# Gate and up projection of two feed-forward stages by seven products of quarters

## The chip, the cores and the metric

The kernel runs on one core of a Trainium2 chip. The metric is the device time of one execution in microseconds (us); the time before is 2174.57 us, the median of three runs from 2169.86 to 2176.21. The engines of the core run side by side and each works through its own queue in order: TensorE (PE, the matmuls; PEld are its weight loads), VectorE (DVE), ScalarE (ACT), GpSimd (POOL) and SyncE (SP), which issues the loads.

## The reference

Three layers on 512 tokens of 1024 features in float32: a recurrent mixer and a feed-forward stage, an attention mixer and a feed-forward stage, then a block with a mixer of its own and a mixture of experts. The change concerns the two feed-forward stages (`layer` 0 and 1), with D_MODEL = 1024 and D_FF = 2816:

```python
def rmsnorm(x, g):
    xf = x.astype(jnp.float32)
    y = xf * lax.rsqrt(jnp.mean(xf * xf, axis=-1, keepdims=True) + EPS)
    return (y * g.astype(jnp.float32)).astype(x.dtype)

def swiglu(h, w_gu, w_down):
    u = h @ w_gu
    g, v = u[..., :D_FF], u[..., D_FF:]
    return (jax.nn.silu(g) * v) @ w_down
...
        h = h + swiglu(rmsnorm(h, norm_g[layer, 1]), ffn_w_gu[layer], ffn_w_down[layer])
```

## The kernel before

Activations lie transposed: eight tiles `h[k]` of 128 features by 512 tokens. Every product in float32 is made of three matmuls on parts: `split` (L422) makes a high part on ACT (a copy that rounds, L425) and a low part on DVE (the difference, L426), and `mm3` (L414) adds high x high, high x low and low x high into one PSUM bank. The gain of the norm is multiplied into the activations when they are split (`normed`, L634), the row factor `rbc` only after the product; its sum of squares is added up on POOL (`square_acc`, L437).

Weights come through `Stream`. `weight_order` lists the weight tiles of the whole kernel in the order of use, 1024 columns each (eight tiles of 128 x 128). `next` splits up to `ahead` = 3 tiles beyond the one in use (`_split`: high part `whi` on ACT at L271, low part `wlo` on DVE at L272, four buffers each) and loads two more; a load brings two tiles, 1 MB, into one of three `raw` buffers on SP's queue.

`ffn` (L789) works in two halves of 11 hidden tiles. For a tile `f`, `product` makes gate and up, 24 matmuls of 512 columns each. Then DVE multiplies both by `rbc` out of PSUM (L813, L816), ACT applies Silu, DVE multiplies them (L817), and `split` makes the parts `hidh` and `hidl`. After a half, its down projection follows: eight residual tiles of 33 matmuls (88 weight tiles), each added to `h[m]` on DVE (L826). The order on each engine comes from a scheduler that works from this code; waits are semaphores between the engines' queues.

Of the kernel before, what the change touches and what calls it, by code (L numbers as in the profile page):

```python
# [22 lines left out]
P = 128  # L23
T = 512
# [7 lines left out]
HF = 11  # L32
# [174 lines left out]

def ffn_layout(gu, dn):
    g = tiles_seq(gu, 0, D, 0, DFF)
    v = tiles_seq(gu, 0, D, DFF, 2 * DFF)  # L210
    return (np.stack([g, v], 1).reshape(2 * NF, P, 8 * P),
            np.concatenate([tiles_seq(dn, 0, HF * P, 0, D), tiles_seq(dn, HF * P, DFF, 0, D)], 0))

# [10 lines left out]
class Stream:  # L224
# [5 lines left out]
    def __init__(self, kb, order, ahead=3, raw_ahead=2):  # L230
        self.kb, self.order, self.ahead, self.raw_ahead = kb, order, ahead, raw_ahead
        self.raw, self.part = {}, {}
        self.stop = len(order) - KD
        self.i = self.ld = self.sp = 0

    def load(self, first=None, r=None):

        name, idx, _ = self.order[self.ld]
        src = self.kb.A[name]
        p, w = src.shape[1], src.shape[2]  # L240
        kb = self.kb
        n = 1
# [14 lines left out]
    def _split(self):  # L257
# [3 lines left out]
        name, idx, gain = self.order[self.sp]  # L261
        r = self.raw.pop(self.sp)
# [21 lines left out]

    def _ready(self, i):

        return self.order[i][0] not in self.LATE or i < self.ld

    def next(self, name):
        assert self.order[self.i][0] == name, (self.order[self.i], name)  # L290
        while self.sp < min(len(self.order), self.stop) and self.sp <= self.i + self.ahead and self._ready(self.sp):
            self._split()
        while self.ld < len(self.order) and self.ld <= self.i + self.ahead + self.raw_ahead and self._ready(self.ld):
# [93 lines left out]
class Kernel:  # L387
# [140 lines left out]

    def ffn_order(self, add, layer):
        for half in range(2):  # L530
            add(f"w_gu{layer}", 22 * half, 22 * half + 22)
            add(f"w_dn{layer}", 11 * half, 11 * half + 11)
# [255 lines left out]

    def ffn(self, layer, gain):  # L789
        nc, W = self.nc, self.W  # L790
        with ExitStack() as ctx:
            kp = ctx.enter_context(self.pool(f"fk{layer}"))
            wk = ctx.enter_context(self.pool(f"fw{layer}"))
            xs = self.normed(self.vec(gain), lambda: wk.tile([P, T], F32, name="fa", bufs=3))
            ssq, rbc = self.ssq, None
            for half in range(2):
                hid, banks = [], {}

                def product(f):
                    banks[f] = [self.bank() for _ in range(2)]  # L800
                    for o in banks[f]:
                        self.mm3(o, list(zip(W.tiles(f"w_gu{layer}", 8), xs)))

                for f in range(HF):
                    if f not in banks:
                        product(f)
# [1433 lines left out]
```

## Time and profile before

| | us |
|---|---|
| median of three runs | 2174.57 |
| the profiled execution, its own time | 2176.83 |
| its span | 2175.1 |
| PE busy | 2089.9 (96%) |
| DVE busy | 1069.7 (49%) |
| ACT busy | 789.2 (36%) |
| POOL busy | 295.9 (14%) |
| layer 0: gate and up, first half | 265.2 to 387.9 |
| layer 0: down, first half | 387.9 to 447.8 |
| layer 0: gate and up, second half | 447.8 to 568.6 |
| layer 0: down, second half | 568.6 to 628.5 |
| layer 1, the same four | 1077.6 to 1201.6, to 1261.5, to 1382.4, to 1442.3 |

A stage's place is read from the matmuls: those on `xh` and `xl` are gate and up, those on `hidh` and `hidl` the down projection. A matmul's record begins when it enters the array and ends when its result is there, so records overlap, and what a matmul costs is the distance to the next one's start. Of the other engines, an instruction that waits in front of its operands can stand in the trace with the wait in its record.

### The profile page before, as it was taken

To read this page: it belongs to the slowest core of one execution; us is meant where nothing else is said; L and a number is where in the kernel's file an instruction comes from. 1 tells how busy PE (TensorE), PEld (TensorE's weight loads), DVE (VectorE), ACT (ScalarE), POOL (GpSimd) and SP (SyncE) were. 2 spreads that over 40 slices of the span, in tenths; PEclk is the share of its full clock that TensorE was granted. 3 is DMA by queue.
4 is the path that set the end of the run, shared out by engine and by line. 5 is a ranking of instruction groups with operands and counts; after the bars stand their busy time and mean duration, and the time that the engine had idled before them with its cause. 6 is when DMAs were issued, how large, how long until landed. Compare 5 with 4: busy or idle time off the path is not lost. (4 is left out here: it accounts for less than half of the span.)

```text
span 2175.1 us, 25890 instructions
## 1 busy us (share of the span) xinstructions
PE 2089.9 (96%) x10282; PEld 1628.4 (75%) x10282; DVE 1069.7 (49%) x1928; ACT 789.2 (36%) x1188; POOL 295.9 (14%) x394
## 2 busy tenths in 40 slices
PE   7999999999999999999999999999999997998987
PEld 5777788888889978888778888888888885332456
DVE  6987744344457464555454344435664433212136
ACT  4675533223347533323432223343453221111223
POOL 2221200000013021211200000030110111111203
PEclk9999999999999999999999999999999998999999
DMA  5122342322224300101032222232211275999971
GB/s 182 47 96 78 120 152 96 107 97 97 88 66 136 133 35 15 40 20 40 19 109 94 97 97 97 88 116 87 88 59 65 97 307 199 371 420 417 380 289 39
DMA packets 71251, 281.72 MB, mean 130 GB/s; under 512 B 8859, under 2 KB 14235, under 8 KB 58452
## 3 DMA queue, kind: packets, MB, share of 16 engines
q1 hardware_dynamic: 60388, 264.63, 33.3%
q0 software_dynamic: 5504, 12.30, 1.5%
q10 hardware_dynamic: 5232, 3.07, 0.5%
q8 instruction: 83, 1.36, 0.2%
q14 instruction: 44, 0.36, 0.1%
HBM read 272.40 MB, written 15.73 MB: 132 GB/s over the span
## 5 line engine op out<-in xcount | busy, mean ns | idle before, releaser
L271 ACT ACTIVATE whi<-raw 128x1024 fp32r<-128x1024 f32 (+2 forms) x249 | 261.5, 1054 | 652.5 <-PE bank L418 587.5
L418 PE MATMUL bank<-xh,whi 128*128 128x512 f32 x1160 | 464.8, 401 | 10.5 <-ACT xh L428 7.6
L418 PE MATMUL bank<-xh,wlo 128*128 128x512 f32 x1160 | 459.1, 396 | 13.4 <-DVE wlo L272 13.3
L418 PE MATMUL bank<-xl,whi 128*128 128x512 f32 x1160 | 455.0, 392 | 0.0
L272 DVE TENSOR_TENSOR wlo<-raw,whi 128x1024 fp32r<-128x1024 f32 (+2 forms) x249 | 310.1, 1249 | 200.0 <-ACT whi L271 194.5
L418 PEld LDWEIGHTS bank<-xh,wlo 128*128 128x128 f32 x1160 | 219.9, 190 | 66.3 <-DVE wlo L272 15.8
L418 PEld LDWEIGHTS bank<-xh,whi 128*128 128x128 f32 x1160 | 220.8, 190 | 57.5 <-ACT xh L428 7.6
L418 PEld LDWEIGHTS bank<-xl,whi 128*128 128x128 f32 x1160 | 220.2, 190 | 49.5 <-issue 1.2
L445 POOL TENSOR_TENSOR ssq<-ssq,sq 128x512 f32<-128x512 f32 x27 | 40.2, 1489 | 791.5 <-ACT sq L432 791.5
L418 PE MATMUL bank<-hidh,whi 128*128 128x512 f32 x352 | 137.2, 390 | 0.0
L418 PE MATMUL bank<-hidh,wlo 128*128 128x512 f32 x352 | 137.1, 390 | 0.0
L418 PE MATMUL bank<-hidl,whi 128*128 128x512 f32 x352 | 137.1, 389 | 0.0
L2043 PE MATMUL bank<-rawa,xe 128*64 128x512 f32 x328 | 93.6, 627 | 9.9 <-DMA rawa<-w_eg 6.2
L432 ACT ACTIVATE prob<-bank 128x512 f32<-128x512 f32 (+1 forms) x96 | 57.1, 595 | 111.1 <-PE bank L1232 81.1
L816 DVE TENSOR_TENSOR fb<-bank,rows 128x512 f32<-128x512 f32 x44 | 30.4, 691 | 133.2 <-PE bank L418 133.2
L1215 PEld LDWEIGHTS acc<-v,prob 128*128 128x128 f32 x640 | 79.8, 192 | 6.2 <-POOL prob L1242 2.2
L1215 PE MATMUL acc<-v,prob 128*128 128x96 f32 x640 | 82.2, 275 | 1.4 <-POOL prob L1242 1.4
L418 PEld LDWEIGHTS bank<-hidl,whi 128*128 128x128 f32 x352 | 66.1, 188 | 13.9
L418 PEld LDWEIGHTS bank<-hidh,wlo 128*128 128x128 f32 x352 | 66.1, 188 | 13.7
L418 PEld LDWEIGHTS bank<-hidh,whi 128*128 128x128 f32 x352 | 66.1, 188 | 13.6
L813 DVE TENSOR_TENSOR fa<-bank,rows 128x512 f32<-128x512 f32 x44 | 30.4, 691 | 88.5 <-PE bank L418 88.5
L975 PE MATMUL bank<-whi,xh 128*128 128x512 f32 (+2 forms) x192 | 71.6, 373 | 0.0
(562 smaller groups left out, 3634.5 us busy)
## 6 DMA issues: line engine op xcount, KB each, us to landing
raw<-w_gu SPq DMA_DIRECT2D x44, 1024.0 KB, 4.8
rawa<-w_eg SPq DMA_DIRECT2D x41, 1024.0 KB, 13.9
raw<-w_dn SPq DMA_DIRECT2D x20, 1024.0 KB, 4.8
raw<-w_eg SPq DMA_DIRECT2D x16, 1024.0 KB, 13.5
rawa<-w_ed SPq DMA_DIRECT2D x16, 1024.0 KB, 14.6
raw<-w_mix SPq DMA_DIRECT2D x12, 1024.0 KB, 4.8
raw<-w_ed SPq DMA_DIRECT2D x10, 1024.0 KB, 15.7
rawb<-w_eg SPq DMA_DIRECT2D x7, 1024.0 KB, 16.9
```

The lines of the kernel that those rows point to most:

```text
L271: nc.scalar.activation(hi, r, AF.Copy)
L272: nc.vector.tensor_tensor(lo, r, hi.bitcast(F32), op=ALU.subtract)
L418: i = nc.tensor.matmul(o, a, b, start=first and n == 0, stop=last and n == N - 1)
L432: return self.nc.scalar.activation(o, i, f, **kw)
L445: self.nc.gpsimd.tensor_tensor(self.ssq, self.ssq, sq, op=ALU.add)
L813: nc.vector.tensor_tensor(a, og, rbc, op=ALU.mult)
L816: nc.vector.tensor_tensor(b, ov, rbc, op=ALU.mult)
L975: nc.tensor.matmul(banks[tt][:, :n], xh, wh, start=k == 0, stop=False)
L1215: i = nc.tensor.matmul(a[:, h * AW:h * AW + AW], e[:K, h * P:h * P + P], v, start=first and h == 0, stop=last and h == HPG - 1)
L2043: last = nc.tensor.matmul(o[s], xe[:, 4 * pi + k, s], w(k), start=pi == 0 and k == 0, stop=pi == 1 and k == 3)
```

## The change

Gate and up are computed for pairs of column tiles (256 columns of the weights) and pairs of feature tiles by one level of Strassen's algorithm in the form with seven products. The weight block of a feature pair and a column pair has four quarters A11, A12, A21, A22 of 128 x 128; the activations of a feature pair have four quarters of 128 features by 256 tokens, B11 to B22.

- `quarters` lays the weights out so that one load of 1 MB (`raw`, 2048 columns) brings the four quarters of a column pair, 512 columns each, for all four feature pairs.
- `operand_sums` makes four differences T1 to T4 of the activations on DVE, once a stage; the seven operands of each feature pair are split, 28 tiles (`xh`, `xl`, and twelve more, `xq`) instead of eight pairs. Before, the gain was multiplied in by `split`; now ACT makes a scaled copy first.
- `_quarter` makes four sums of weight quarters (`qsum`, S1 to S4) on POOL, with three buffers, and splits each of the seven operands, 512 columns, as before on ACT and DVE (L497, L498). `tno` numbers pairs of quarters, so that `ahead` = 3 counts three pairs, six products.
- `quarter_products` runs the seven products (12 matmuls of 256 columns each, four feature pairs by three parts), and combines them: two copies out of PSUM on ACT, five sums out of PSUM on DVE and two sums on POOL (L902). In a stage's first step, three products run on the first three feature pairs before the last pair is needed.
- In `ffn`, the gate's product with `rbc` moves from PSUM to SBUF on DVE (L987), the up's to POOL (L989).
- The hidden tiles come in chunks of 8, 8 and 6 (`CHUNKS`) instead of 11 and 11. `ffn_steps` puts the gate of the next pair ahead of a chunk's down projection; the last chunk's starts with the tiles that don't need the last pair (`down_tiles`, `LATE`).

```diff
+CHUNKS = (8, 8, 6)
+LATE = 3
...
 class Stream:
     def load(self, first=None, r=None):
...
+        if isinstance(gain, str):
+            if (name, idx) not in self.quarters:
+                r = kb.wp.tile([P, 2048], F32, name="raw", bufs=kb.RAW)
+                kb.nc.sync.dma_start(r, src[idx])
+                self.quarters[name, idx] = {c: r[:, 512 * i:512 * i + 512] for i, c in enumerate(("A11", "A12", "A21", "A22"))}
+            self.ld += 1
+            return
...
+    SUMS = {"S1": ("A21", "A22", ALU.add), "S2": ("S1", "A11", ALU.subtract), "S4": ("A12", "S2", ALU.subtract), "S3": ("A11", "A21", ALU.subtract)}
+
+    def _quarter(self, q, c):
+        kb, nc = self.kb, self.kb.nc
+        if c in self.SUMS:
+            a, b, op = self.SUMS[c]
+            q[c] = self.sums.tile([P, 512], F32, name="qsum", bufs=3)
+            nc.gpsimd.tensor_tensor(q[c], q[a], q[b], op=op)
...
+        kb.split(hi, lo, q[c])
...
     def next(self, name):
-        while self.sp < min(len(self.order), self.stop) and self.sp <= self.i + self.ahead and self._ready(self.sp):
+        while self.sp < min(len(self.order), self.stop) and self.tno[self.sp] <= self.tno[self.i] + self.ahead and self._ready(self.sp):
             self._split()
...
+    PRODUCTS = {"A11": "B11", "A12": "B21", "S1": "T1", "S2": "T2", "S4": "B22", "S3": "T3", "A22": "T4"}
+
+    def ffn_steps():
+        out, lo = [], 0
+        for c, n in enumerate(CHUNKS):
+            hi = (lo + n) // 2
+            out += [(x, j) for j in range(lo // 2, hi) for x in "gu" if (x, j) not in out]
+            if hi < NF // 2:
+                out.append(("g", hi))
+            out.append(("d", c))
+            lo += n
+        return out
...
+    def quarter_products(self, name, xs, wk, out, late):
...
+        for c in self.PRODUCTS:
...
+            if c in ("A11", "S1"):
+                m[c] = copied(o)
+            elif c == "A12":
+                sum_(o, m["A11"], x=a[0])
+            elif c == "S2":
+                m[c] = sum_(o, m["A11"])
+                m["U4"] = sum_(m[c], m["S1"], nc.gpsimd)
+            elif c == "S4":
+                sum_(o, m["U4"], x=a[1])
+            elif c == "S3":
+                m[c] = sum_(o, m["S2"])
+                sum_(m[c], m["S1"], nc.gpsimd, b[1])
+            else:
+                sum_(o, m["S3"], x=b[0])
...
     def ffn(self, layer, gain):
...
+            for j in range(KD // 2):
+                scaled = tiles("fa", 4)
+                for i in range(2):
+                    self.act(scaled[i], self.h[2 * j + i], AF.Copy, scale=g[:, 2 * j + i:2 * j + i + 1])
+                q = self.operand_sums(tiles("fb", 2), *scaled)
+                xs.append({})
+                for n in self.PRODUCTS.values():
+                    xs[j][n] = room.pop(0), room.pop(0)
+                    self.split(*xs[j][n], q[n])
+            for k in range(KD):
+                self.square_acc(k, self.h[k], lambda: wk.tile([P, T], F32, name="fa", bufs=4))
...
+                if kind == "u":
+                    for f, a, b in zip((2 * i, 2 * i + 1), gates.pop(i), out):
+                        nc.vector.tensor_tensor(a, a, rbc, op=ALU.mult)
+                        self.act(a, a, AF.Silu)
+                        nc.gpsimd.tensor_tensor(b, b, rbc, op=ALU.mult)
+                        nc.vector.tensor_tensor(a, a, b, op=ALU.mult)
+                        hid[f] = [kp.tile([P, T], FR, name=f"hid{x}", bufs=max(CHUNKS)) for x in "hl"]
+                        self.split(*hid[f], a)
```

The order on DVE in the middle of layer 0's gate and up, before: one hidden tile, with two weight tiles for a later one (`rows` is `rbc`).

```order
L813 TENSOR_TENSOR fa_2375<-bank_2315,rows_2223 128x512
L272 TENSOR_TENSOR wlo_2346<-raw_2279,whi_2345 128x1024
L816 TENSOR_TENSOR fb_2378<-bank_2316,rows_2223 128x512
L817 TENSOR_TENSOR fa_2375<-fa_2375,fb_2378 128x512
L272 TENSOR_TENSOR wlo_2388<-raw_2279,whi_2387 128x1024
L426 TENSOR_TENSOR hidl_2382<-fa_2375,hidh_2381 128x512
```

The same place of after on DVE: part of the step of an up product, with the low parts for the next step's gate and up among the sums out of PSUM (L902).

```order
L498 TENSOR_TENSOR wlo_3035<-qsum_3032,whi_3034 128x512
L498 TENSOR_TENSOR wlo_3035<-qsum_3038,whi_3034 128x512
L902 TENSOR_TENSOR fc_3054<-bank_3031,fc_3013 128x256
L990 TENSOR_TENSOR fa_2795<-fa_2795,fb_2938 128x512
L902 TENSOR_TENSOR fb_2939<-bank_3057,fc_3054 128x256
L498 TENSOR_TENSOR wlo_3091<-raw_2631,whi_3090 128x512
L498 TENSOR_TENSOR hidl_3076<-fa_2795,hidh_3075 128x512
L990 TENSOR_TENSOR fa_2796<-fa_2796,fb_2939 128x512
L498 TENSOR_TENSOR wlo_3091<-raw_2804,whi_3090 128x512
```

Two operations of 1024 columns have become low parts of 512, seven for a step, and the products with `rbc` and of gate and up now have both inputs in SBUF. POOL has nothing in this place before; what stands in its queue around layer 0's stage is this (the sums of squares of the stage, a clearing of a buffer, then the sums of squares after the stage):

```order
L445 TENSOR_TENSOR ssq_2064<-ssq_2064,fa_2078 128x512
L445 TENSOR_TENSOR ssq_2064<-ssq_2064,fa_2081 128x512
L569 MEMSET z_2022 128x1024
L570 DMA yd_104<-z_2022 128x8x1024
L445 TENSOR_TENSOR ssq_2064<-ssq_2064,fa_2084 128x512
L445 TENSOR_TENSOR ssq_4419<-ssq_4419,sq_4421 128x512
```

After, POOL in the middle of the gate and up of layer 0, nearly two steps:

```order
L334 TENSOR_TENSOR qsum_2991<-raw_2631 128x512
L334 TENSOR_TENSOR qsum_2997<-qsum_2991,raw_2631 128x512
L902 TENSOR_TENSOR fa_2796<-fc_2911,fc_2855 128x256
L334 TENSOR_TENSOR qsum_3032<-raw_2631,qsum_2997 128x512
L334 TENSOR_TENSOR qsum_3038<-raw_2631 128x512
L334 TENSOR_TENSOR qsum_3131<-raw_2804 128x512
L902 TENSOR_TENSOR fc_3015<-fc_3013,fc_2988 128x256
L989 TENSOR_TENSOR fb_2938<-fb_2938,rows_2485 128x512
L334 TENSOR_TENSOR qsum_3167<-qsum_3131,raw_2804 128x512
L334 TENSOR_TENSOR qsum_3173<-raw_2804,qsum_3167 128x512
L902 TENSOR_TENSOR fb_2939<-fc_3054,fc_2988 128x256
L989 TENSOR_TENSOR fb_2939<-fb_2939,rows_2485 128x512
```

Sums for a later step stand between those that combine this step's products, and each waits in its place. At the start of layer 0's stage, DVE now has this behind the last residual addition (`h7`), of which the last rows are the twelve low parts of the later operands:

```order
L837 TENSOR_TENSOR h7_83<-h7_83,bank_1962 128x512
L498 TENSOR_TENSOR wlo_2197<-raw_1756,whi_2196 128x512
L498 TENSOR_TENSOR wlo_2197<-raw_1805,whi_2196 128x512
L498 TENSOR_TENSOR xq0_2042<-fb_2106,xq0_2042 128x256
L498 TENSOR_TENSOR xq1_2043<-fb_2106,xq1_2043 128x256
...
L888 TENSOR_TENSOR fb_2130<-fa_2126 128x256
L888 TENSOR_TENSOR fb_2131<-fa_2127,fa_2126 128x256
L888 TENSOR_TENSOR fb_2130<-fa_2127,fb_2130 128x256
L498 TENSOR_TENSOR xq5_2047<-fa_2126,xq5_2047 128x256
...
L498 TENSOR_TENSOR xq11_2053<-fb_2131,xq11_2053 128x256
```

Before, one low part of 512 columns stood there. On POOL, the seven sums of squares of the stage have moved from between the residual additions to behind the last of them.

## Rows read from the trace of the kernel before

**Rows 1.** The page's first part: engine, busy us, share of the span, instructions.
```profile
PE 2089.9 (96%) x10282; PEld 1628.4 (75%) x10282; DVE 1069.7 (49%) x1928; ACT 789.2 (36%) x1188; POOL 295.9 (14%) x394
```

**Rows 2.** Stretches: length, then PE, PEld, DVE, ACT, POOL; clock, DMA, GB/s.
```profile
265.20:387.90 122.70, 122.70 (x540) 100.55 (x539) 55.55 (x71) 39.96 (x50) 3.80 (x4) 1.00 0.36 129
447.80:568.60 120.80, 120.80 (x529) 99.18 (x528) 54.22 (x64) 35.33 (x43) 0.00 (x0) 1.00 0.28 96
1077.60:1201.60 124.00, 122.89 (x539) 100.45 (x538) 60.01 (x74) 43.63 (x56) 10.87 (x7) 1.00 0.27 94
1261.50:1382.40 120.90, 120.90 (x530) 99.24 (x529) 54.22 (x64) 35.40 (x43) 0.00 (x0) 1.00 0.28 96
```

**Rows 3.** Timeline of PE in gate and up: start, length, instruction.
```profile
329.72 0.39 PE L418 MATMUL bank<-xl,whi 128*128 128x512 f32 x1
...
351.70 0.39 PE L418 MATMUL bank<-xl,whi 128*128 128x512 f32 x1
```

**Rows 4.** Timeline of PE, matmuls of 256 columns in two other places.
```profile
1505.57 0.28 PE L418 MATMUL bank<-rqh,rkh 128*128 128x256 f32 x1
1505.69 0.28 PE L418 MATMUL bank<-rql,rkh 128*128 128x256 f32 x1
...
1575.06 0.28 PE L1622 MATMUL bank<-whi,xh 128*128 128x256 f32 x1
...
1578.92 0.28 PE L1623 MATMUL bank<-wlo,xh 128*128 128x256 f32 x1
```

**Rows 5.** Groups by form: count | busy us, mean ns of one | idle before.
```profile
L271 ACT ACTIVATE whi<-raw 128x1024 fp32r<-128x1024 f32 x237 | 249.8, 1058 | 638.8 <-PE bank L418 582.5 <-issue 17.9 <-PE bank L977 14.1
L426 DVE TENSOR_TENSOR oTl<-bank,oTh 128x256 fp32r<-128x256 f32 x16 | 6.7, 417 | 11.1 <-ACT oTh L425 11.1
L1259 POOL TENSOR_TENSOR av<-av 128x256 f32<-128x256 f32 x15 | 11.0, 733 | 45.4 <-DVE av L1198 45.2
```

**Rows 6.** Timelines of POOL and DVE at the kernel's end (xN: merged).
```profile
2148.23 12.77 POOL L2214 TENSOR_TENSOR rawa<-rawa,rows 128x512 f32<-128x512 f32 x8 [16.38 <-ACT rows L432]
...
2149.56 3.46 DVE L2183 SCALAR_TENSOR_TENSOR raw<-raw,rawa 128x512 f32<-128x512 f32 x2 [4.01 <-POOL rawa L2214]
2152.95 3.49 DVE L2184 SCALAR_TENSOR_TENSOR raw<-raw,h 128x512 f32<-128x512 f32 x2
...
2163.52 1.29 DVE L2183 SCALAR_TENSOR_TENSOR raw<-raw,rawa 128x512 f32<-128x512 f32 x2 [0.17 <-ACT raw L432]
2164.73 1.29 DVE L2184 SCALAR_TENSOR_TENSOR raw<-raw,h 128x512 f32<-128x512 f32 x2
```

**Rows 7.** Timelines of POOL and DVE at the kernel's start.
```profile
17.38 1.29 POOL L445 TENSOR_TENSOR ssq<-ssq,y 128x512 f32<-128x512 f32 x1
19.34 4.83 POOL L445 TENSOR_TENSOR ssq<-ssq,y 128x512 f32<-128x512 f32 x3 [0.67 <-ACT y L432]
...
20.75 4.50 DVE L272 TENSOR_TENSOR wlo<-raw,whi 128x1024 fp32r<-128x1024 f32 x2
```

**Rows 8.** Timelines of POOL and DVE ahead of layer 0's feed-forward stage.
```profile
245.26 1.82 POOL L445 TENSOR_TENSOR ssq<-ssq,fa 128x512 f32<-128x512 f32 x1 [21.53 <-ACT fa L432]
...
244.69 1.23 DVE L272 TENSOR_TENSOR wlo<-raw,whi 128x1024 fp32r<-128x1024 f32 x1 [0.20 <-ACT whi L271]
245.84 0.68 DVE L744 TENSOR_TENSOR h<-h,bank 128x512 f32<-128x512 f32 x1
```

**Rows 9.** Timeline of all engines at the start of layer 0's stage.
```profile
265.42 0.69 DVE L744 TENSOR_TENSOR h<-h,bank 128x512 f32<-128x512 f32 x1 [1.21 <-PE bank L418]
...
267.74 1.59 POOL L445 TENSOR_TENSOR ssq<-ssq,fa 128x512 f32<-128x512 f32 x1
```

**Rows 10.** Timeline of PE behind a wait, ahead of layer 1's stage.
```profile
1064.03 0.44 PE L1263 MATMUL bank<-ident,av 128*128 128x128 f32 x2 [2.11 <-DVE av L1259]
...
1066.57 0.63 PE L418 MATMUL bank<-oTh,whi 128*128 128x512 f32 x1
1066.99 0.63 PE L418 MATMUL bank<-oTl,whi 128*128 128x512 f32 x1
```

More of the change, by code (lines that the diff above doesn't have):

```diff
@@ L232, in __init__ @@
         self.raw, self.part = {}, {}
+        self.tno, t, half = [], -1, False
+        for _, _, gain in order:
+            quarter = isinstance(gain, str)
+            t += not (quarter and half)
+            half = quarter and not half
+            self.tno.append(t)
+        self.quarters, self.sums, self.half = {}, None, None
         self.stop = len(order) - KD
@@ L236, in load @@
     def load(self, first=None, r=None):
-        name, idx, _ = self.order[self.ld]
+        name, idx, gain = self.order[self.ld]
         src = self.kb.A[name]
@@ L261, in _split @@
         name, idx, gain = self.order[self.sp]
+        if isinstance(gain, str):
+            return self._quarter(self.quarters[name, idx], gain)
+        self.half = None
         r = self.raw.pop(self.sp)
@@ new lines, in ffn, with tiles @@
+            W.sums = wk
+            def tiles(name, bufs):
+                return [wk.tile([P, T], F32, name=name, bufs=bufs) for _ in range(2)]
+            room = [self.xp.tile([P, T], FR, name=f"x{i}{k}") for k in range(KD) for i in "hl"]
+            room += [kp.tile([P, T], FR, name=f"xq{i}") for i in range(7 * KD // 2 - len(room))]
+            room = [x[:, hf * i:hf * i + hf] for x in room for i in range(2)]
+            g = self.vec(gain)
+            xs = []
+            for j in range(KD // 2):
[7 more added lines that the diff above has]
+                    self.split(*xs[j][n], q[n])
@@ new lines, in ffn @@
+            for k in range(KD):
+                self.square_acc(k, self.h[k], lambda: wk.tile([P, T], F32, name="fa", bufs=4))
+            ssq, rbc = self.ssq, None
+            gates, hid, lo = {}, {}, 0
+            for u, (kind, i) in enumerate(self.ffn_steps()):
+                if kind == "d":
+                    tl, bank = W.tiles(f"w_dn{layer}", KD * CHUNKS[i]), {}
+                    hi = lo + CHUNKS[i]
+                    for (k, m), wt in zip(down_tiles()[i], tl):
+                        if k == lo:
+                            bank[m] = self.bank()
+                        self.mm3(bank[m], [(wt, hid[k])], first=k == lo, last=k == hi - 1)
+                        if k == hi - 1:
+                            nc.vector.tensor_tensor(self.h[m], self.h[m], bank[m], op=ALU.add)
+                    lo = hi
+                    continue
+                out = tiles(*(("fa", 4) if kind == "g" else ("fb", 2)))
+                self.quarter_products(f"w_gu{layer}", xs, wk, out, u == 0)
+                if kind == "g":
+                    gates[i] = out
+                if u == 0:
+                    rcol = self.rms_cols(ssq)
+                if u == 1:
+                    rbc = self.to_rows(rcol)
+                if kind == "u":
[6 more added lines that the diff above has]
+                        self.split(*hid[f], a)
@@ L829, in rope @@
+            W.sums = None
     def rope(self, x, tt, heads, wk, eng):
```

119 lines of the change are left out of this document (79 added, 40 removed).

## The prediction, made before the changed kernel was run

> **What bounds the kernel now.** I read the page's head first. TensorE (PE) is busy 96% of the span [rows 1]: as long as PE is fed, the span moves only where PE's own work moves. Then I read the four gate and up stretches of the two feed-forward stages [rows 2]. They last 122.7, 120.8, 124.0 and 120.9 us; PE is busy in all of them at full clock (1.00, the 2.4 GHz level), VectorE (DVE) 55.6, 54.2, 60.0 and 54.2 us, and GpSimd (POOL) 3.8, 0.0, 10.9 and 0.0 us. So before the change these stretches are PE's alone, DVE has half of its time free, and POOL does nothing but the sums of squares.
>
> The length of a matmul record holds its latency, so what one costs is read from start to start. From 329.72 to 351.70 lie 96 matmuls of 512 columns [rows 3], 0.229 us each. A layer has 1056 of them for gate and up: 241.8 us, against the 243.5 us of its two stretches in layer 0.
>
> **What the change takes off PE.** I call a step what the new code does for one pair of column tiles of gate or up: seven products of 12 matmuls with 256 columns, 84 in all, where two tiles took 48 matmuls of 512 columns, 48 x 0.229 = 10.99 us. A layer has 22 steps. The trace has matmuls of 256 columns: 34 of them from 1575.06 to 1578.92, 0.1135 each, and two at 1505.57 and 1505.69, 0.12 [rows 4]. I take 0.116: 84 x 0.116 = 9.74 us a step, 214 us a layer (209.8 by 0.1135, 221.8 by 0.12). PE gains 22 x 1.25 = 27 us a layer, if it is fed. The down projection keeps its 528 matmuls of 512 columns a layer, only in three chunks; its weights are split as before. Eight more residual additions a layer lie on DVE while it is half idle. I cost that at nothing. The loads are the same 1 MB a step on SP's queue into the same three buffers, and the DMA engines are busy 0.27 to 0.36 of the time there [rows 2].
>
> **What it puts on the other engines.** In a step, by the order of after:
> - ScalarE (ACT): 7 high parts of 512 columns, two copies of 256 out of PSUM, one Silu and one high part of a hidden tile. A high part of 1024 takes 1.058 us [rows 5]; with 0.53 for each of the eleven, the short ones too, 5.8 us. No bound.
> - DVE: 10 operations of 512 columns with both inputs in SBUF (7 low parts of weights, the low part of a hidden tile, the gate by rbc, gate times up), and 5 sums of 256 columns with one input in PSUM. Two operations of the first kind in a row stand at 2163.52 and the next at 2164.73 [rows 6]: 0.605 each. One of the second kind is recorded with 0.417 [rows 5]; since records overlap by 0.08 (0.69 recorded for 0.605), it costs 0.34. 10 x 0.605 + 5 x 0.34 = 7.75 us.
> - POOL: 4 sums of weight quarters and one product of up with rbc, of 512 columns, and two sums of 256. With 1.29 us for 512 [rows 7] and 0.73 for 256 [rows 5]: 5 x 1.29 + 2 x 0.73 = 7.9 us.
>
> Each of them alone is below PE's 9.74. Together they are not, for DVE and POOL hold each other up. At the end of the kernel both have a queue of operations with two SBUF inputs [rows 6]: 8 of POOL take 12.77 us, and DVE's start at 2149.56 and 2152.95, two each, 1.70 us for one, where it needs 0.605 alone. So one of each takes 1.70 together, and POOL's share is 1.70 - 0.605 = 1.10. The very operation that the change multiplies shows the same: two low parts of 1024 columns (`wlo<-raw,whi`) take 4.50 us between three sums of POOL [rows 7], and one alone 1.23 [rows 8]. An operation that reads PSUM is not held: `h<-h,bank` takes its 0.68 us inside a POOL sum that runs from 245.26 for 1.82 us [rows 8]. For a POOL sum of 256 columns I estimate 1.10 - (1.29 - 0.73) = 0.54.
>
> In a step the two must therefore take turns for 5 x 1.10 + 2 x 0.54 + 10 x 0.605 = 5.50 + 1.08 + 6.05 = **12.63 us**, more than PE's 9.74 and more than the 10.99 of before. That is the lower bound: the five PSUM sums (1.70 us) all lie under POOL's turns. If none do, it is 14.33. Both queues run in order: DVE's low part of a sum waits for ACT, which waits for POOL; POOL's next sum waits for one of three buffers, which DVE frees; the gate-times-up on DVE waits for two POOL operations in a row. So some turns are lost, and I take the middle, 13.5.
>
> The Trainium skill ("SBUF — State Buffer", "SBUF: two separate sides") calls the port pair of the two engines an exclusive lock, held for the whole instruction, against which the other fully blocks. With whole records as turns a step would be 5 x 1.29 + 2 x 0.73 + 10 x 0.69 = 14.8 us; the rows agree that one blocks the other, but give 1.70 and not 1.98 for a pair, and the measurement decides.
>
> **What is hidden.** The weights are split three pairs of products ahead. The six first products of each of the three chunks are thus ready when PE comes to it, their work done under the down projection or the stage ahead, where POOL is idle: 4 x 1.10 + 6 x 0.605 = 8.0 us a chunk, 24 a layer. At a chunk's end the two sums of POOL of its last step (1.08) slip into the down projection, and one low part of 1024 comes in (1.14, 1.23 less the overlap): even. PE's products run behind DVE's low parts, so its 9.74 lie inside.
>
> **The start of a stage.** Before, after the last residual addition at 265.42 only one low part and one sum of squares (267.74) were to come [rows 9], and PE did not stop. Now 16 DVE operations of 256 columns (4 differences, 12 low parts; 16 x 0.34 = 5.4 us) and all seven sums of squares on POOL (7 x 1.10 = 7.7 us) follow it. The three products that run ahead on three of four pairs cover 27 x 0.116 = 3.1 us. At best PE waits 3 us; at worst all of it but the cover comes on top, 5.4 + 7.7 - 3.1 = 10, and up to 3 more if PE's clock falls in the wait. I take 8.
>
> **The sum.** A layer: 22 x 13.5 - 24 + 8 = 281 us, where 243.5 stood: +37.5. Layer 1's stretches are 1.4 us longer before, which I leave. Two layers: +75. The profiled execution took 2176.83 us (span 2175.1), 2.3 more than the median 2174.57; 2176.8 + 75 = 2251.8, on the median's scale **2250 us**, 3.5% slower. With the lower ends, 22 x 12.63 - 24 + 3 = 257, +13 a layer, 2201. With the upper, 22 x 14.33 - 24 + 13 = 304, +61 a layer, 2296.
>
> **Rivals.**
> - *PE stays the bound.* If POOL's turns came into gaps of DVE, each engine would fit into 9.74 and PE's saving would be real: 22 x 9.74 + 3 = 217, -26 a layer, 2122 us. The condition is that a step's turns sum to less than 9.74; from 11.8 down (22 x 11.8 - 24 + 8 = 243.6, the length of before) the change gains. For it: POOL is idle in these stretches now and DVE half idle [rows 2]. Against it: rows 6 and 7, with the same operation. I give it 10%.
> - *Whole records as turns*, the step of 14.8 us: 22 x 14.8 - 3 x (4 x 1.29 + 6 x 0.69) + 8 = 306, +62 a layer, 2299 us. It decides if operations that don't wait in full queues pay their set-up each time. For it: the order above is full of such waits; against it: 1.70 for a pair. 8%. This is the time by the lock as the Trainium skill's page "SBUF — State Buffer" ("SBUF: two separate sides") states it.
> - *No change to be told*, within 0.3% (6.5 us, about what a measurement of this kernel can tell from no change): a step would have to come out near 11.8, under the 12.63, with turns lost nowhere and more hidden under the down projection than I count. 4%.
> - *PE's clock falls.* After a wait that ended at 1064.03, with 2.11 us idle, matmuls of 512 columns stand 0.43 apart [rows 10], the 1.2 GHz level. If the waits of each product did that, 84 x 0.232 = 19.5 us would bound a step: 22 x 19.5 = 429, +185 a layer, 2545 us. A step of 13.5 leaves 3.8 us of waiting in seven pieces of 0.5; no row of mine has the low level behind a wait that short. 2%.
>
> **How the numbers follow.** Forecast 76%, PE-bound 10%, whole records 8%, no change 4%, clock 2%. The range reaches from 2190, below the lower ends' 2201, to 2310, over the whole records' 2299: it leaves out 16%. Faster by over 0.3%: 0.10; within: 0.04; slower by over 0.3%: 0.86.
>
> **What would show it.** In the gate and up stretches of after: PE's busy time falls under the stretch's length, in gaps before products whose releaser is a low part on DVE; low parts of 512 columns on DVE come out near 1.7 us instead of 0.69 and POOL's sums near 1.7 instead of 1.29; a step takes 13 to 14 us; DVE and POOL are both near full there. The down projections stay at 0.227 to 0.229 a matmul. The stage's start shows a gap of 3 to 6 us. It is wrong if the low parts keep 0.69 while POOL works (then PE bounds, and the time is near 2122), or if a step's first products after a down projection are not ready (then 24 us a layer are lost again).

## The result, and the profile after

The changed kernel takes 2298.58 us (median of four runs, 2294.06 to 2300.78) against 2173.12 for the kernel before (four runs): a ratio of 1.0575, 95% interval 1.055 to 1.060. It is slower by 5.75%. The profiled execution took 2296.61 us (span 2294.9), 119.8 more than the profiled one of before.

The page's first part, against [rows 1]: PE's share falls from 96% to 91% with 1580 more instructions (84 short matmuls a step in place of 48), and POOL's time is 2.4 times what it was.

```profile
PE 2098.4 (91%) x11862; PEld 1703.5 (74%) x11866; DVE 1327.4 (58%) x2412; ACT 909.3 (40%) x1552; POOL 718.0 (31%) x702
```

The stretches of gate and up of both layers, which answer to [rows 2], and then the first down projection of layer 0 (length, then PE, PEld, DVE, ACT, POOL; clock, DMA, GB/s). A stage now has three chunks, of 9, 8 and 5 steps.

```profile
265.02:398.76 133.74, 102.73 (x767) 98.52 (x765) 101.58 (x146) 58.74 (x116) 88.20 (x62) 0.90 0.28 102
444.83:545.59 100.76, 85.78 (x674) 83.76 (x673) 66.32 (x106) 40.56 (x79) 60.66 (x47) 0.97 0.22 75
591.14:650.45 59.31, 52.64 (x422) 51.83 (x421) 39.34 (x64) 25.23 (x49) 32.17 (x25) 0.97 0.23 74
1139.71:1277.46 137.75, 108.57 (x767) 101.60 (x766) 116.91 (x178) 68.11 (x139) 92.42 (x64) 0.89 0.20 68
1324.83:1427.04 102.21, 86.97 (x673) 84.87 (x672) 67.31 (x108) 40.84 (x80) 61.09 (x47) 0.95 0.23 78
...
```
```profile
398.76:444.83 46.07, 45.54 (x192) 37.21 (x193) 21.25 (x27) 11.95 (x17) 13.77 (x9) 0.96 0.28 95
...
```

The row left out of the first fence, the last chunk of layer 1, is 59.27 us long; the other two down projections of layer 0 are 45.55 and 37.36. Gate and up: 293.8 us in layer 0 (243.5 before) and 299.2 in layer 1 (244.9): +50.3 and +54.3. Down projections: 129.0 and 127.2 (119.8 each): +9.2 and +7.4. The rest comes to -1.4. So all of the loss lies in the two stages.

**A chunk in the middle of a stage.** What PE waits for in the second chunk of layer 0, and what DVE waits for (us in total, times, longest):

```profile
PE bank L490 <- DVE wlo L498: 14.9, 9, 2.2
```
```profile
DVE fa L990 <- POOL fb L989: 15.3, 7, 3.5
DVE fa L902 <- POOL fc L902: 8.4, 3, 2.8
DVE fa L987 <- POOL fa L902: 7.1, 3, 2.4
```

PE waits only for low parts of weights on DVE. DVE waits 30.8 us for results of POOL. In 7.8 us of that chunk the timelines of DVE and of POOL (start, length, instruction) show both ways in which one holds the other up:

```profile
479.19 2.83 DVE L498 TENSOR_TENSOR wlo<-qsum,whi 128x512 fp32r<-128x512 f32 x2
481.93 0.41 DVE L902 TENSOR_TENSOR fb<-bank,fc 128x256 f32<-128x256 f32 x1
485.80 0.69 DVE L990 TENSOR_TENSOR fa<-fa,fb 128x512 f32<-128x512 f32 x1 [3.46 <-POOL fb L989]
```
```profile
479.01 1.30 POOL L334 TENSOR_TENSOR qsum<-raw 128x512 f32<-128x512 f32 x1 [3.58 <-DVE wlo L498]
480.26 1.20 POOL L902 TENSOR_TENSOR fc<-fc 128x256 f32<-128x256 f32 x1
481.42 1.74 POOL L334 TENSOR_TENSOR qsum<-raw 128x512 f32<-128x512 f32 x1
483.24 1.29 POOL L334 TENSOR_TENSOR qsum<-qsum,raw 128x512 f32<-128x512 f32 x1
484.49 1.28 POOL L989 TENSOR_TENSOR fb<-fb,rows 128x512 f32<-128x512 f32 x1
```

The two low parts at 479.19 take 2.83 us under two POOL operations, where two alone take 1.29 [rows 6]; the sums out of PSUM keep their 0.41. Then DVE stands for 3.46 us, since its next instruction needs the product of up with rbc, and POOL has two sums of weights to do ahead of that product. POOL had stood for 3.58 before, behind DVE. Taken from the records of all instructions of the chunk, DVE or POOL is at work in 98.2 of its 100.8 us, both at once in 28.8. That fits turns but does not show them; the experiments below do.

**The start of a stage.** What PE waits for up to its third step, in layer 0 (265 to 313) and in layer 1 (1140 to 1185):

```profile
PE bank L490 <- ACT xq L497: 11.0, 1, 11.0
PE bank L542 <- DVE dg L540: 5.0, 1, 5.0
PE bank L524 <- POOL ssq L517: 3.8, 1, 3.8
```
```profile
PE bank L490 <- ACT whi L497: 6.8, 2, 5.9
...
```

With the shorter waits that are left out, layer 1 comes to 15.0 us, against 19.8 in layer 0. What is left of the two stretches goes in part with PE's clock, which is granted at 0.74 and 0.77 of full speed there: PE is busy 28.0 and 29.7 us, where two steps take 20.1 in a chunk without waits.

```profile
265.02:312.90 47.88, 28.02 (x179) 26.65 (x178) 27.70 (x49) 20.15 (x42) 29.39 (x21) 0.74 0.35 132
1139.71:1184.53 44.82, 29.71 (x179) 26.06 (x178) 37.28 (x73) 28.08 (x62) 25.80 (x17) 0.77 0.14 48
```

In layer 0 the 11.0 us are a wait of ACT for memory: the tiles `xq` lie where the tile of zeros `z` of the pool ahead lay, and the transfer out of it was still running.

```profile
281.40 0.72 ACT L497 ACTIVATE xq<-fb 128x256 fp32r<-128x256 f32 x2 [10.05 <-DMA yd<-z]
```

In layer 1 no such wait shows. There the residual tiles come 1.40 us apart (two rows of additions below). DVE stands idle for 0.71 us ahead of each, and the differences and splits of all four pairs, 44 operations from 1140.51 to 1155.6, come behind the last one in its queue. The squares then wait for their sums on POOL, seven in 11.93 us, and ACT has the first weights' high parts behind them. Timelines of DVE and POOL:

```profile
1138.51 0.69 DVE L1269 TENSOR_TENSOR h<-h,bank 128x512 f32<-128x512 f32 x1 [0.71 <-PE bank L490]
1139.91 0.69 DVE L1269 TENSOR_TENSOR h<-h,bank 128x512 f32<-128x512 f32 x1 [0.71 <-PE bank L490]
1140.51 0.42 DVE L888 TENSOR_TENSOR fb<-fa 128x256 f32<-128x256 f32 x1
...
1154.80 0.75 DVE L498 TENSOR_TENSOR xq<-fb,xq 128x256 fp32r<-128x256 f32 x2
```
```profile
1153.91 11.93 POOL L517 TENSOR_TENSOR ssq<-ssq,fa 128x512 f32<-128x512 f32 x7 [27.98 <-ACT fa L504]
```

**The start of a down projection.** PE's timeline at 398.76: a wait for its first weights, and some matmuls of 512 columns 0.43 apart, the 1.2 GHz level, where 0.227 is usual.

```profile
398.76 0.50 PE L490 MATMUL bank<-hidh,whi 128*128 128x512 f32 x1 [2.45 <-ACT whi L311]
...
402.08 0.63 PE L490 MATMUL bank<-hidh,wlo 128*128 128x512 f32 x1
402.51 0.63 PE L490 MATMUL bank<-hidh,whi 128*128 128x512 f32 x1
```

### The profile page after: what moved, and what is told of

It is laid out like the page before. It is cut to its first block, busy times and chain, and to the rows that moved or that the text cites. A ratio compares the mean times of both kernels' runs of the same rounds, so it can differ in the third digit from the quotient of the medians.

```text
span 2294.9 us, 30664 instructions
## 1 busy us (share of the span) xinstructions
PE 2098.4 (91%) x11862; PEld 1703.5 (74%) x11866; DVE 1327.4 (58%) x2412; ACT 909.3 (40%) x1552; POOL 718.0 (31%) x702
## 5 line engine op out<-in xcount | busy, mean ns | idle before, releaser
L490 PE MATMUL bank<-xh,whi 128*128 128x256 f32 (+1 forms) x1160 | 333.9, 337 | 20.5 <-ACT xh L500 8.3
L490 PE MATMUL bank<-xh,wlo 128*128 128x512 f32 (+1 forms) x808 | 287.8, 357 | 62.5 <-DVE wlo L498 50.1
L490 PE MATMUL bank<-xl,whi 128*128 128x256 f32 (+1 forms) x1160 | 329.0, 333 | 3.6 <-ACT whi L497 1.6
L312 DVE TENSOR_TENSOR wlo<-raw,whi 128x1024 fp32r<-128x1024 f32 (+2 forms) x161 | 203.9, 1271 | 84.3 <-ACT whi L311 80.3
L490 PEld LDWEIGHTS bank<-xh,wlo 128*128 128x128 f32 x808 | 156.8, 194 | 92.0 <-DVE wlo L498 58.1
L490 PE MATMUL bank<-xq,whi 128*128 128x256 f32 x1056 | 212.6, 292 | 12.4 <-ACT xq L497 11.6
L334 POOL TENSOR_TENSOR qsum<-raw 128x512 f32<-128x512 f32 x88 | 129.7, 1482 | 295.6 <-DVE wlo L498 226.3
L490 PEld LDWEIGHTS bank<-xq,whi 128*128 128x128 f32 x1056 | 170.8, 198 | 13.6 <-ACT xq L497 12.1
L498 DVE TENSOR_TENSOR wlo<-qsum,whi 128x512 fp32r<-128x512 f32 x176 | 158.2, 929 | 8.1 <-ACT whi L497 8.0
L490 PE MATMUL bank<-xq,wlo 128*128 128x256 f32 x528 | 154.1, 292 | 0.0
L497 ACT ACTIVATE whi<-qsum 128x512 fp32r<-128x512 f32 x176 | 105.1, 624 | 105.2 <-POOL qsum L334 75.2
L498 DVE TENSOR_TENSOR wlo<-raw,whi 128x512 fp32r<-128x512 f32 x134 | 110.7, 850 | 4.7 <-ACT whi L497 4.5
```

The lines of the kernel that those rows point to most:

```text
L312: nc.vector.tensor_tensor(lo, r, hi.bitcast(F32), op=ALU.subtract)
L334: nc.gpsimd.tensor_tensor(q[c], q[a], q[b], op=op)
L490: i = nc.tensor.matmul(o, a, b, start=first and n == 0, stop=last and n == N - 1)
L497: nc.scalar.activation(hi, src, AF.Copy)
L498: return nc.vector.tensor_tensor(lo, src, hi.bitcast(F32), op=ALU.subtract)
```

## Experiments: what feeds PE

All twelve kernels that were run stand in this section and the next two. The theory: turns of DVE and POOL set a step. The rivals: PE is slower on short matmuls than I took it to be, or DVE's queue or its waiting in order is what costs. The measure is the second chunk of layer 0, eight steps, 100.76 us in the changed kernel.

**The sums of quarters left out.**

```diff
-            q[c] = self.sums.tile([P, 512], F32, name="qsum", bufs=3)
-            nc.gpsimd.tensor_tensor(q[c], q[a], q[b], op=op)
+            q[c] = q[a]
```

> The changed kernel without the four sums of weight quarters a step: raw quarters are split in their place, so the values are not those of the reference; every matmul, split, copy and PSUM sum stays. Theory, DVE and POOL take turns and the turns set the step: they fall to 1.10 + 2 x 0.54 + 10 x 0.605 = 8.2 us, under PE's 84 x 0.116 = 9.74, so a step comes to about 9.8 (12.4 with the sums), a stage of gate and up to about 230 us (293.8 and 299.2), the down projections lose their late starts (about 121 instead of 129.0 and 127.2), and the total comes to about 2150 us. Rival one, the chain through DVE, ACT and POOL at each hidden tile is what PE waits for: the step stays above 11.5, the total above 2255. Rival two, matmuls of 256 columns with a new bank every 12 cost PE more than 0.116 each: PE has no gaps, and its spacing comes out above 0.125.

2162.1 us, ratio 0.9946 (0.9929 to 0.9963). The stretches of the first down projection and of the second chunk:

```profile
363.56:407.11 43.55, 43.55 (x195) 36.04 (x193) 18.59 (x25) 9.84 (x14) 2.73 (x2) 1.00 0.27 97
407.11:487.37 80.26, 80.26 (x673) 80.26 (x672) 63.35 (x109) 41.80 (x82) 24.63 (x22) 1.00 0.31 105
```

PE has no gap: 672 matmuls in 80.26 us are 0.1194 each, 10.03 a step. So PE's own work is not what makes the changed kernel's chunk 100.8 us, though each matmul costs 0.0034 more than the 0.116 I took. The down projection is back at its length, too. The total fell less than the 2150 expected, because the starts stayed long: in layer 1 PE waited 9.7 us for the sums of squares.

**All of POOL's work on DVE.**

```diff
-            nc.gpsimd.tensor_tensor(q[c], q[a], q[b], op=op)
+            nc.vector.tensor_tensor(q[c], q[a], q[b], op=op)
...
-                        nc.gpsimd.tensor_tensor(b, b, rbc, op=ALU.mult)
+                        nc.vector.tensor_tensor(b, b, rbc, op=ALU.mult)
```

(and the two sums of 256 likewise)

> The changed kernel with all of a step's POOL work (four sums of quarters, one product with rbc for up, two sums of 256) moved to DVE; the same arithmetic. Theory, turns: without POOL, DVE alone needs 15 x 0.605 + 7 x 0.34 = 11.5 us a step, less than the 12.63 that the two take together, so the kernel gets faster although DVE has more to do: a step of 11.5 instead of 12.4, low parts near 0.68 us each, a stage near 255 to 275, the total 2200 to 2250. Rival, DVE's own queue sets the step and POOL only delays it little: 3.7 us more on DVE make a step of 16, a stage near 375, the total near 2455.

2178.1 us, ratio 1.0013 (1.0004 to 1.0023): 120 us off, with seven more operations a step on DVE. Second chunk:

```profile
415.76:497.33 81.57, 80.98 (x673) 80.41 (x672) 79.58 (x153) 44.18 (x82) 0.00 (x0) 1.00 0.30 104
```

DVE does 153 operations in 81.57 us, where with POOL beside it it did 106 in 100.76. That can't be if DVE's own load set the step. I had expected a step of 11.5 us and 2200 to 2250; it is faster than that. Part of each chunk's DVE work falls into the down projections, and DVE (98% busy) and PE come out nearly even.

**Parts of it.** First only the sums of quarters on DVE (the first of the two edits above), then only the work on finished tiles (the second edit and the sums of 256), and that last one also with sums of quarters that are computed on POOL and not read:

```diff
-            q[c] = self.sums.tile([P, 512], F32, name="qsum", bufs=3)
-            nc.gpsimd.tensor_tensor(q[c], q[a], q[b], op=op)
+            s = self.sums.tile([P, 512], F32, name="qsum", bufs=3)
+            nc.gpsimd.tensor_tensor(s, q[a], q[b], op=op)
+            q[c] = q[a]
```

> The changed kernel with the four sums of weight quarters on DVE, but the product of up with rbc and the two sums of 256 still on POOL. Theory, turns: a step costs DVE 14 x 0.605 + 5 x 0.34 = 10.2 us and POOL's turns 1.10 + 2 x 0.54 = 2.2 more, 12.35, or 10.65 where the sums out of PSUM lie under POOL: the second chunk's eight steps, less 6 to 9 us done ahead, come to 82 to 93 us (100.8 in the changed kernel, 81.6 with all on DVE), the total to 2185 to 2235. Rival, what costs is the way of each hidden tile over POOL (three engines in a row) and not the turns of the weight sums: it stays near 100 us a chunk and above 2270.

> The same with the sums of quarters read as in the changed kernel: they stay on POOL, the product with rbc and the sums of 256 are on DVE. Theory of turns: the same 11.7 to 13.4 a step as with sums that nobody reads, the chunk 86 to 99 us and within 4 us of that kernel. Rival: ACT and DVE must wait for each sum, so the chunk is longer than with unread sums by more than 4 us; or, if only waits for POOL at the finished tiles cost, it is 80 to 82 us and the total 2175 to 2185, like the kernel with all on DVE.

> The changed kernel with the work on finished tiles (the product with rbc, the two sums of 256) on DVE, so that DVE waits for no result of POOL; POOL still computes the four sums of quarters a step, but nothing reads them, raw quarters are split in their place, and the values are not the reference's. Theory, the two engines hold each other up also where neither needs the other's result: 11 x 0.605 + 7 x 0.34 = 9.0 us of DVE and 4 x 1.10 = 4.4 of POOL make 11.7 to 13.4 a step, the second chunk (eight steps, 8.0 us done ahead) 86 to 99 us, the total 2200 to 2290. Rival, what cost was DVE's waiting in order for POOL's results (30.8 of the 100.8 us of that chunk in the changed kernel): without a result to wait for, DVE's 9.0 lie under PE's 10.0, and the chunk takes 80 to 81 us, the total stays below 2180.

In that order 2222.5 us (ratio 1.0214, 1.0186 to 1.0242), 2240.0 (1.0297, 1.0280 to 1.0315) and 2230.9 (1.0258, 1.0241 to 1.0275). The second chunk of each:

```profile
422.66:510.29 87.63, 83.58 (x673) 82.05 (x672) 80.84 (x131) 40.58 (x78) 30.84 (x22) 0.98 0.28 95
```
```profile
435.60:525.96 90.36, 83.40 (x673) 80.78 (x672) 87.39 (x129) 41.65 (x80) 37.88 (x25) 1.00 0.26 87
```
```profile
438.76:526.96 88.20, 82.52 (x673) 80.65 (x672) 85.22 (x131) 41.16 (x81) 33.28 (x20) 1.00 0.28 95
```

All three lie where the turns put them: 82 to 93, 86 to 99, 86 to 99. The third decides against the rival: no result of POOL is waited for there, DVE's own 9.0 us a step would lie under PE's 10.0, and still the chunk is 7.9 us longer than PE's floor of 80.26. Its timelines show where that comes from:

```profile
472.15 6.11 POOL L334 TENSOR_TENSOR qsum<-raw 128x512 f32<-128x512 f32 x4 [6.69 <-DMA raw<-w_gu]
```
```profile
472.46 1.53 DVE L990 TENSOR_TENSOR fb<-fb,rows 128x512 f32<-128x512 f32 x1
473.92 0.41 DVE L903 TENSOR_TENSOR fc<-bank,fc 128x256 f32<-128x256 f32 x1
474.25 1.44 DVE L499 TENSOR_TENSOR wlo<-raw,whi 128x512 fp32r<-128x512 f32 x1
475.62 1.51 DVE L903 TENSOR_TENSOR fb<-fc 128x256 f32<-128x256 f32 x1
477.05 1.76 DVE L499 TENSOR_TENSOR wlo<-raw,whi 128x512 fp32r<-128x512 f32 x1
478.73 0.41 DVE L903 TENSOR_TENSOR fb<-bank,fc 128x256 f32<-128x256 f32 x1
```

Under four POOL sums DVE needs 6.27 us (472.46 to 478.73) for what alone takes 3 x 0.605 + 2 x 0.34 = 2.50: 0.94 us lost a sum, near the 1.10 that I took from [rows 6]. The whole chunk says the same: DVE is busy 85.2 us with operations that take 66.6 alone, beside 20 sums, 0.93 lost for each. With the sums read, the chunk is 2.2 us longer (90.4 against 88.2), and 25 of POOL's sums lie in it in place of 20. From 90.4 to the 100.8 of the changed kernel three operations go from DVE to POOL. By turns that is 8 x (1.10 + 2 x 0.54 - 0.605 - 2 x 0.34) = 7.2 us; the other 3 can be DVE's waiting in order for POOL's results, which no run isolates.

## Experiments: the starts and the chunks

**Squares earlier, and zeros apart.** In the first kernel the squares and sums of a pair stand behind that pair's splits; in the second the tile of zeros lives until the first stage ends.

```diff
                     self.split(*xs[j][n], q[n])
-            for k in range(KD):
-                self.square_acc(k, self.h[k], ...)
+                for k in (2 * j, 2 * j + 1):
+                    self.square_acc(k, self.h[k], ...)
```
```diff
-        self.ffn(0, "n01")
+            self.ffn(0, "n01")
```

> The changed kernel with the squares and their seven sums on POOL put behind each pair of residual tiles instead of behind all splits. Theory, the sums of squares are one of the things that make the stage's start long (47.9 us to PE's third step in layer 0 and 44.8 in layer 1, against 2 x 12.4): the starts get 5 to 8 us shorter each, the total 2280 to 2288. Rival, the start is set by the splits of the normed input and of the first weights, which are not moved: the starts stay within 2 us, the total at 2297 or above.

> The changed kernel with the tile of zeros kept until the end of the first feed-forward stage, so that the operand tiles of the stage no longer lie in its memory. Theory, the 11.3 us in which PE waits at the start of layer 0's stage, ended by a high part on ACT that waited for the transfer out of the tile of zeros, goes, and the start comes down from 47.9 to about 38 us, the total to about 2287. Rival, the splits and sums behind that wait are due anyway: the start comes to the 44.8 of layer 1 at best, the total to 2294 or more. Layer 1 does not change by either.

Squares earlier: 2299.4 us, starts of 46.6 and 44.0 us (47.9 and 44.8). The rival is right: in the same two queues, the sums cost the same at another place. Zeros apart: the start of layer 0 comes down to 39.9 us, as expected, but the seven steps behind it take 88.6 in place of 85.9, and the total, 2298.2 (2288.9 to 2301.2), can't be told from the changed kernel's. The execution in the trace is the fastest of the four, 2288.9.

**The start edited alone.** The sums of quarters and the tiles' work stay on POOL; squares are emitted behind the first eight products and summed on DVE, the root mean square's columns, diagonal and rows come later, zeros are kept.

```diff
+                sq = self.ssq if first else wk.tile([P, T], F32, name="sq2", bufs=2)
+                self.act(sq, src, AF.Square)
+                if not first:
+                    nc.vector.tensor_tensor(self.ssq, self.ssq, sq, op=ALU.add)
...
-                if u == 0:
-                    rcol = self.rms_cols(ssq)
-                if u == 1:
-                    rbc = self.to_rows(rcol)
+                if u == 1:
+                    rcol, held = self.rms_cols(self.ssq), (i, out)
+                elif u == 2:
+                    rbc = self.to_rows(rcol, dg=diag[0])
+                    gated(*held)
```

> The changed kernel, its sums of weight quarters, product with rbc and sums of 256 on POOL as they are, with only the start edited: squares one by one behind the first eight products and summed on DVE, columns of the root mean square behind the second step, diagonal behind the first product of the third, rows behind the third, zeros kept through the first stage. Theory, the start is a cost of its own beside the turns: the third step ends 8 to 15 us earlier in each layer and most of it stays, the total 2268 to 2285. Rival, DVE and POOL work at their turns from the stage's first sum on, and PE only waits elsewhere: the total stays at 2290 or above.

2279.3 us, ratio 1.0481 (1.0465 to 1.0497): 19 us less than the changed kernel. The first chunks of both layers:

```profile
264.58:380.30 115.72, 99.62 (x767) 95.99 (x766) 102.13 (x149) 54.89 (x110) 78.64 (x56) 0.95 0.33 117
1122.51:1256.58 134.07, 108.83 (x767) 102.07 (x765) 120.89 (x185) 68.01 (x139) 81.31 (x57) 0.90 0.21 70
```

18.0 us less in layer 0, 3.7 in layer 1. So in layer 0 the start was a cost of its own, three waits in a row; in layer 1 the edits hardly help. What remains there is the input's 44 operations and then, I take it, the turns.

**The chunks alone**, in the kernel before:

```diff
-            for half in range(2):
+            for n in CHUNKS:
```

> The kernel before with the down projection in chunks of 8, 8 and 6 and nothing else of the change. Theory, the 8 us that each layer's down projections got longer in the changed kernel come from PE's supply by DVE and not from the chunks: 2172 to 2178 us, the down projections together within 2 us of 119.8 a layer. Rival, each start of a chunk costs a wait for the first weights of the down projection and a while at the lower clock: two starts become three, 127 us a layer, 2182 to 2190.

2173.0 us, ratio 0.9999 (0.9986 to 1.0011). Its down projections:

```profile
349.38:392.94 43.56, 43.56 (x193) 36.05 (x192) 16.52 (x18) 9.15 (x10) 0.00 (x0) 1.00 0.28 97
...
590.36:623.11 32.75, 32.75 (x146) 27.04 (x145) 21.68 (x44) 19.08 (x43) 7.74 (x6) 1.00 0.21 69
```

119.87 us, PE busy in all of it. The chunks cost nothing; the 8 us a layer come with PE's supply.

## Experiments: a version that gains

**All sums on DVE with the start edited**, first with the diagonal still made at the third step's end, then with the diagonal behind that step's first product:

```diff
                 if not squares:
+                    if rcol is not None and not diag:
+                        diag.append(self.diagonal(rcol))
                     return
```

> All sums on DVE, and three edits at the start of a stage: each square is emitted behind one of the first eight products and summed on DVE in place of POOL, the columns of the root mean square come behind the second step and the rows behind the third, and the tile of zeros is kept through the first feed-forward stage. Theory, in layer 1 PE's gaps of 7.2 us (a high part of weights on ACT behind squares that wait for POOL) and of 4.3 us (the diagonal on DVE) go, in layer 0 those of 2.0 and 3.3: starts of 48 and 35 us become about 37 and 31, the total 2160 to 2166, under the kernel before. Rival, the start is DVE's queue and nothing else: it has the same operations and seven more, and the total stays at 2176 or above.

> All sums on DVE with the edits at the start as before, and the diagonal tile (four operations on DVE) put behind the first product of the third step, while PE's matmul on it stays at that step's end. Theory, the waits of 5.5 and 7.3 us for the diagonal, which stood at the end of DVE's queue, and the two of 1.0 behind each go: starts shorter by 7 and 9 us, the total 2153 to 2160. Rival, PE gives the time back a few products later because DVE is the bound in the whole first chunk (its 11.3 us a step against PE's 10.0): the total stays within 4 us of 2170.7.

2170.7 us (ratio 0.9979, 0.9967 to 0.9991), then 2170.0 (0.9979, 0.9969 to 0.9989). The first falls between theory and rival. In the second the rival is right: the waits for the diagonal, 5.2 and 7.0 us, are gone, but PE waits 3.4 us longer in each layer for low parts a few products later, and the first chunks end only 1.3 and 2.5 us earlier, counted from the stage's start.

**One operation of each hidden tile moved** to the down projections, on top of that:

```diff
-                    nc.vector.tensor_tensor(b, b, rbc, op=ALU.mult)
...
-                            nc.vector.tensor_tensor(self.h[m], self.h[m], bank[m], op=ALU.add)
+                            d = wk.tile([P, T], F32, name="sq2", bufs=2)
+                            nc.vector.tensor_tensor(d, bank[m], rbc, op=ALU.mult)
+                            nc.vector.tensor_tensor(self.h[m], self.h[m], d, op=ALU.add)
```

> The kernel with all sums on DVE and the start edited, with one operation of a hidden tile moved: up is no longer multiplied by rbc (44 operations of 512 columns on DVE, in the gate and up steps), the down projection's sums are, before they are added to the residual (48 products out of PSUM on DVE, during the down projections). The same result by another order of products. Theory, DVE's 11.3 us a step against PE's 10.0 set the first chunk; with 10.7 a step, over its seven steps behind the start, each layer's first chunk gets 4 to 6 us shorter, and the DVE work added to the down projections is hidden there: the total 2157 to 2164. Rival, the first chunk is set by something else (ACT, or the transfers of the quarters), or the longer residual additions hold up the next stage: the total within 3 us of 2170 or above it.

2160.5 us, ratio 0.9943 (0.9925 to 0.9960): 0.57% faster than the kernel before. The first chunk behind its third step and the second chunk, then the first products of the attention stage:

```profile
292.58:357.54 64.96, 62.84 (x507) 60.88 (x506) 63.90 (x124) 39.00 (x71) 0.00 (x0) 1.00 0.25 83
401.08:481.35 80.27, 80.27 (x674) 80.26 (x672) 78.54 (x150) 45.02 (x83) 0.00 (x0) 1.00 0.32 106
607.73:625.63 17.90, 13.08 (x49) 10.08 (x48) 13.64 (x32) 7.60 (x23) 5.62 (x15) 0.90 0.16 45
```

and the first of these in the kernel without this edit (its products of the attention stage take 11.47 us, from 614.82 to 626.29):

```profile
293.00:364.56 71.56, 66.11 (x512) 62.08 (x510) 70.50 (x134) 40.98 (x73) 0.00 (x0) 1.00 0.24 79
```

With the 1.7 us of six down matmuls taken off the 71.56, the first chunk is 4.9 us shorter, as expected, and the second stands on PE's floor of 80.3. But the longer residual additions hold up the stage behind layer 0 by 6.4 us, as the rival had it.

## Why the prediction was right, and where it was off

The forecast was 2250 us, slower, in a range of 2190 to 2310; the chunk lengths that it implies can be set against the rows one by one. That the total fell into the range is luck: 2298.6 lies 2 us above the upper end of my own sum, 2296, and inside only because I had put its end over a rival's 2299.

- **The step, 13.5 us with 8.0 hidden a chunk: right.** The second chunk should take 8 x 13.5 - 8 = 100.0 us and the third 5 x 13.5 - 8 = 59.5. They took 100.8 and 102.2, 59.3 and 59.3. PE's last four steps in layer 0's first chunk can be read directly, 13.5 us each at full clock:

```profile
344.67:398.76 54.09, 42.95 (x338) 40.65 (x336) 46.71 (x64) 23.34 (x46) 36.24 (x26) 1.00 0.27 93
```

In that stretch 17 operations of POOL and 44 of DVE with 512 columns start, 8 of POOL with 256, and 21 sums out of PSUM: by my turns 49.6 to 56.8 us. The runs uphold the mechanism: POOL's work on DVE brings the second chunk to 81.6, and sums on POOL that nobody reads keep it at 88.2, though DVE then has four operations a step fewer. That the middle of 12.63 and 14.33 fits so well is in part luck. In the second chunk PE's first two steps and the last take 10.0 us and the five between them 14.1: more is hidden than my 8.0, the steps behind it cost more than 13.5, and the two cancel.
- **The start of a stage, 8 us: the mis-sized term.** The first chunk should take 9 x 13.5 - 8 + 8 = 121.5 us and took 133.7 and 137.8: the start cost 20.2 and 24.2. In layer 0 I had not seen that `xq` would lie in the memory of `z` (11.0 us), nor priced the diagonal, on which PE waits in order (5.0); the sums of squares, which I had priced, hold PE for 3.8 more. In layer 1 I let three of four pairs be ready, from rows of layer 0; there the tiles come 1.40 us apart and all 44 operations follow, not 16. For a lower clock I had allowed 3 us, and in both starts PE is busy 8 to 10 us longer, the columns' matmuls included, than two steps take elsewhere. My upper bound, 13, was too low for both.
- **The down projection, nothing: wrong by 9.2 and 7.4 us.** I called DVE half idle there. But a chunk ends with DVE late, and the first weights of the down projection stand behind that on ACT and DVE. The chunks cost nothing, as I said; the supply did. In layer 0 PE waits 4.5 of the 9.2 us; the rest is matmuls that stand further apart, some at the 1.2 GHz level.
- These misses, 12.2 + 16.2 + 9.2 + 7.4 = 45 us, are the difference between the 2251.8 that I summed on the profiled scale and the 2296.6 measured, but for 0.2 us: what else moved nearly cancels.
- **PE's gain, 1.25 us a step if fed:** it is 10.99 - 10.03 = 0.96, 21 us a layer in place of 27. PE was not the bound, so this did not enter the sum; for the rival in which PE stays the bound it would have.
- **Signs.** Gaps whose releaser is a low part on DVE: right. Low parts near 1.7 us each: only 34 of 310, at 1.65 to 1.79, while 220 keep 0.67 to 0.76; the mean of those out of sums is 0.93. POOL's sums of weights near 1.7: 1.48 to 1.54 on the mean. Down projections at 0.227 to 0.229 a matmul: not at their start, 0.43. "DVE and POOL both near full": wrong, they are 66% and 60% busy in the second chunk. Nor is it a sign of turns that one of the two is nearly always at work: that holds for 76.3 of 80.3 us in the kernel without sums too, where PE never waits. What tells is the length of DVE's records beside POOL's.
- Of the rivals, *PE stays the bound* needed POOL out of DVE's way, and came true only in the kernels that took it away. *Whole records as turns* gave 2299 us, closest to the total, but by luck: its step of 14.8 made up for a start and down projections as wrong as mine. The operations of the four steps above would need 17 x 1.29 + 8 x 0.73 + 44 x 0.69 = 58.1 us by whole records, and they took 54.1; the 0.93 lost a sum says the same. The second chunk alone would not decide: the operations that start in it give 101.1 us by whole records. *No change* needed a step near 11.8. *PE's clock falls* needed the low level behind every product's wait; in those four steps PE waits eight times, for up to 1.9 us, and the granted clock is 1.00.

## What to carry to other kernels

Before work is put on GpSimd because it is idle, add what it takes from VectorE (0.9 to 1.1 us here for a sum of 512 columns) to VectorE's own time, as if they were one engine, wherever both read two operands from SBUF. If that sum passes the step of the bounding engine, expect the move to lose; here doing it all on VectorE was 120 us faster. At the start of a stage, count every operation from the last input to the first product, with what its memory and each engine's queue order make it wait for. A method that cuts one engine's time by 9% gains only as far as the engines that feed it can follow.

## What the runs showed of the hardware

A GpSimd sum stood for long beside short VectorE operations. In the kernel with all sums on DVE, a sum of squares, alone 1.29 us, took 4.63 (timeline of POOL), beside these rows of DVE:

```profile
1085.12 4.63 POOL L517 TENSOR_TENSOR ssq<-ssq,fa 128x512 f32<-128x512 f32 x1 [31.91 <-ACT fa L504]
```
```profile
1085.25 0.43 DVE L498 TENSOR_TENSOR xq<-fa,xq 128x256 fp32r<-128x256 f32 x1
...
1087.93 0.70 DVE L334 TENSOR_TENSOR qsum<-qsum,raw 128x512 f32<-128x512 f32 x1
1088.66 1.63 DVE L334 TENSOR_TENSOR qsum<-raw,qsum 128x512 f32<-128x512 f32 x1
```

Nine DVE operations, each right behind the one before, ran undisturbed from 1085.25 to 1088.63. Then came a pause of 0.03 us, POOL's sum ended 1.12 later, and it was DVE's next operation that was held (1.63 in place of 0.70). The Trainium skill ("SBUF — State Buffer", "SBUF: two separate sides") gives the pair to whichever starts first, for one whole instruction. Here POOL's record starts before all nine, and still the sum ends only behind a pause of DVE's queue. When within its record POOL asked for the pair, the profile doesn't show, and this is one place.

The second is small: matmuls of 256 columns stand 0.1194 us apart in a chunk in which PE never waits (672 in 80.26 us), against 0.1135 in a run of 34 elsewhere [rows 4].
